# A two-block transformer on one core: modulation loads paced over four buffers, an earlier spread of inverse sums, squares added in two chains

## The chip, the core and the metric

One core of one Trainium2 chip runs the whole program. The metric is the device time of one execution in microseconds (us), taken as the median of several runs. TensorE (PE) multiplies, VectorE (DVE), ScalarE (ACT) and GpSimd (POOL) work elementwise, and DMA moves data. DMAs are issued from SyncE's queue (SP) or, here for some tensors, from POOL's. Each engine takes its instructions in order.

## What is computed

The input is 512 positions of width 1024, float32. The first model's two layers (A: attention over the 256 keys picked by an index score; B: attention with decay), each followed by an MLP, feed the second model's two layers (C: grouped attention; G: a gated MLP that mixes positions), again each with an MLP. Cut to what the change touches:

```python
def rms_norm(x, g):
    x32 = x.astype(jnp.float32)
    y = x32 * lax.rsqrt(jnp.mean(x32 * x32, axis=-1, keepdims=True) + EPS)
    return (y * g.astype(jnp.float32)).astype(x.dtype)
...
    cond = jax.nn.silu(c)                      # c: one vector of 1024
    for i in range(DEPTH):                     # two layers
        mod = cond @ ada_w[i] + ada_b[i]       # ada_w[i]: 1024 x 6144
        sh1, sc1, g1, sh2, sc2, g2 = jnp.split(mod, N_MOD, axis=-1)
...
        p = jax.nn.softmax(s, axis=-1).astype(v.dtype)
        return jnp.einsum('bkgqs,bskd->bqkgd', p, v)
```

`mod` depends on `c` alone, not on the positions, so the kernel computes it beside other work: layer 0's during the first model's first MLP, layer 1's during its second MLP.

## The kernel before, in words

**Layout.** The running state is eight tiles `h[0..7]`, 128 features by 512 positions each. Every product is done three times to keep float32 accuracy: each operand is split into a high part (ACT copies it to a rounded type) and a low part (DVE or POOL subtracts), and `mul3` (line 548) multiplies high by high, high by low and low by high. A weight tile (128x1024, 512 KB) is loaded by SP into `wr` (two buffers) and split into `wh` and `wl` (three buffers each).

**An MLP** (`mlp`, line 675) goes over four chunks of 1024 hidden features: eight "up" tiles, whose results pass through `t` (DVE), `a` (ACT), `ah` (ACT) and `al` (DVE), then eight "down" tiles, which read all eight `ah` and `al` and are added into `h` by DVE. A tile is 24 matmuls of 512 columns. In the first model's two MLPs, `step()` (line 681) advances a side task by one step after each tile but every eighth, 49 times in all; what is left of it is drained before the last eight down tiles.

**The side task** (`ada`, line 1236): for each of six column groups `q` and eight row blocks `k`, a 512 KB tile `adaw` of `ada_w` is loaded from POOL's queue, and DVE adds it, times one factor for each partition, into `ada` in two instructions of 512 columns. After the eighth, DVE transposes `ada` into another `adaw` buffer and reduces it into `red`. So one step is one load. At the end 16 small DMAs from POOL gather `red` into `part`, and DVE reduces that to `mod`. `adaw` has two buffers, the default of the MLP's pool.

**Attention heads** (`heads`, line 813) go two at a time. For each head, `softmax` (line 758) makes the logits in PSUM, DVE adds the mask and takes the extreme, and ACT takes the exponential and adds up the sums; `turned` (line 795) transposes on PE and splits; then matmuls with the values add up in the PSUM bank `po`. ACT and DVE bring `po` into `both`. In layers A and C (`late`) the division by the sums comes at the end: `inverses` (line 782) takes reciprocals on DVE, ACT spreads them over 64 columns each (into a tile of the tag `top`, one buffer), and PE transposes them into a `po` bank; then DVE multiplies `both`. The tag `po` has two banks. Layer A calls this 16 times (8 for the first 256 positions, with `narrow`, 8 for the others), layer C 8 times.

**Squares** (`squares`, line 583) serve `rms` (line 601) ahead of layer A, the first MLP, layer B and the second MLP: ACT squares the eight `h` tiles, and DVE adds seven of them one after the other into `acc`; four small matmuls with ones sum over the partitions.

**What sets the order.** The program is recorded, not emitted, by `Sched`. `order` (line 274) then plays a list schedule with its own costs (`cost`, line 243) and latencies: an instruction is placed when its inputs are there, its engine is free, its buffer is free (buffers of a tag are given out strictly in recorded order) and none of lower number is ready. The result is each engine's fixed order of instructions. On the chip the engines wait for one another by semaphores in that order, whatever the planner's clock said. `after` (line 194) adds one predecessor, the instruction recorded last, to all that is recorded within it; it is a predecessor in the planner alone, and the emitted program has no semaphore for it. All instructions are emitted at line 414, so the profile gives that one line and the rows are told apart by tile names.

```python
248:            return 1000 if o.eng == "gpsimd" else 60, 1550 + (x.box[1] - x.box[0]) * x.size * 4 / 360
262:            return (300 + 164 * n if n < 16 else 100 + 2.2 * n), 130
300:                if q["next"] != t.index or not room(t.pool, q):
685:                if side is not None and tiles % 8:
1245:                    w = self.t(pool, "adaw", [P, D])
1246:                    nc.gpsimd.dma_start(w, I["ada_w"][i, k, :, q * D : (q + 1) * D])
```

Line 248 books a load from POOL at 1000 ns of issue and 3006 ns to its landing for 512 KB.

Of the kernel before, what the change touches and what calls it, by code (L numbers as in the profile page):

```python
# [14 lines left out]
ALU = mybir.AluOpType  # L15
AX = mybir.AxisListType
PSUM = bass.MemoryType.PSUM

P = 128
S = 512  # L20
D = 1024
HALVES = slice(0, S // 2), slice(S // 2, S)
KD = D // P
# [15 lines left out]
V_BS = 208  # L39
V_QG, V_KG = 224, 226  # L40
NV = 228


class View:
# [110 lines left out]
class Sched:  # L155
# [37 lines left out]
    @contextmanager  # L193
    def after(self):

        self.gate = len(self.ops) - 1
        yield
        self.gate = None

# [42 lines left out]
    @staticmethod  # L242
    def cost(o, outs, ins):

        ps = any(x.tile.pool.space is not None for x in ins)
        if o.name == "dma_start":
            x = (outs + ins)[0]
            return 1000 if o.eng == "gpsimd" else 60, 1550 + (x.box[1] - x.box[0]) * x.size * 4 / 360
        n = max(x.size for x in outs + ins) if o.name in ("tensor_reduce", "bn_stats", "bn_aggr", "max") else outs[0].size
        if o.eng == "tensor":  # L250
            x = outs[0].size
            if o.name == "matmul" and ins[0].tile.dt == F32:
                return max(64, 4 * 0.42 * x), 200
            return max(107 if o.name == "transpose" else 54, 0.417 * x + 2.5), 200
        if o.eng == "scalar":
            aps = sum(isinstance(o.kw.get(k), View) for k in ("bias", "scale", "accum_out"))
            return (51 if ps else 93) + 0.834 * n + 93 * max(0, aps - 1) + (60 if aps == 1 else 0), 130
        if o.eng == "gpsimd":
            if o.name == "tensor_scalar":
                return 160 if n < 16 else 244 + 0.834 * n, 130  # L260
            if o.name == "memset":
                return 100, 130
            return (300 + 164 * n if n < 16 else 100 + 2.2 * n), 130
        c = 68 + 1.042 * n
        if o.name == "scalar_tensor_tensor" and isinstance(o.args[2], View):
            c += 61
        if o.name == "tensor_scalar" and not ps:
            c = 130 + 0.52 * n
        if o.name == "reciprocal":
            c = 70 + 6.3 * n  # L270
        return c, 130
# [219 lines left out]
class Net:  # L491
# [91 lines left out]
    def squares(self, col=None):  # L583

        nc = self.nc
        acc = self.t(self.np_, "acc", [P, S])
        for k in range(KD):
            kw = {} if col is None else {"scale": self.vec[:, col + k : col + k + 1]}
            sq = acc if k == 0 else self.t(self.np_, "sq", [P, S], bufs=1) if k % 2 else self.t(self.np_, "y", [P, S])
            nc.scalar.activation(sq, self.h[k], AF.Square, **kw)  # L590
            if k:
                nc.vector.tensor_tensor(acc, acc, sq, ALU.add)
        ps = self.po()
        for b in range(NB):
            nc.tensor.matmul(ps[:, 2 * b : 2 * b + 2], acc[:, b * P : (b + 1) * P], self.ones[:, 0:2], start=True, stop=True)
        return ps[:, 0 : 2 * NB : 2]
# [216 lines left out]
    def heads(self, pool, npr, nth, lhs, rhs, v, o, masks=None, causal=True, rows=(None, None), blocks=range(NB), narrow=False, late=False):  # L813


        nc = self.nc
        n = len(blocks) * P
        W = {i: (i + 1) * P if causal else S for i in blocks}
        keys = range(max(W.values()) // P)
        sums = self.t(pool, "sums", [P, 2 * len(blocks)])  # L820
        both = self.t(pool, "o", [P, n], bufs=1)
        for h in range(2):
            pr = self.softmax(pool, npr, lhs[h], rhs[h], W, masks, rows[h], sums, h, late)
            po = self.po()
            for b in keys:
                th, tl, c = self.turned(pool, nth, pr, W, b)
                if narrow:
                    for x, (part, y) in enumerate(((0, th), (0, tl), (64, th))):
                        nc.tensor.matmul(po[0:64, c], v[h][b][:, part : part + 64], y[:, c], start=b == 0 and x == 0, stop=b == keys[-1] and x == 2)
                else:  # L830
                    nc.tensor.matmul(po[:, c], v[h][b], th[:, c], start=b == 0, stop=False)
                    nc.tensor.matmul(po[:, c], v[h][b], tl[:, c], start=False, stop=b == keys[-1])
            r = slice(64 * h, 64 * h + 64)
            if narrow:
                nc.scalar.activation(both[r], po[0:64, :n], AF.Copy)
            else:
                top = self.t(pool, "top", [P, n], bufs=1)[0:64]
                nc.scalar.activation(top, po[0:64, :n], AF.Copy)
                nc.vector.tensor_tensor(both[r], po[64:128, :n], top, ALU.add)
        if late:  # L840
            nc.vector.tensor_tensor(both, self.inverses(pool, sums, len(blocks)), both, ALU.mult)
        self.split(o[0][:, :n], o[1][:, :n], both)

    def attn_out(self, o, w, gate=None, norm=None):
# [391 lines left out]
    def ada(self, i):  # L1236
        nc, I = self.nc, self.I

        def side(pool):
            m = self.mod[i]  # L1240
            red, part = (self.t(pool, x, [P, 4, 6 * KD], bufs=1) for x in ("red", "part"))
            for q in range(6):
                acc = self.t(pool, "ada", [P, D])
                for k in range(KD):
                    w = self.t(pool, "adaw", [P, D])
                    nc.gpsimd.dma_start(w, I["ada_w"][i, k, :, q * D : (q + 1) * D])
                    c = self.cs[:, k : k + 1]
                    for s in (0, 512):
                        a = acc[:, s : s + 512]
                        if k == 0:  # L1250
                            nc.vector.tensor_scalar(a, w[:, s : s + 512], c, 1.0, ALU.mult, ALU.mult)
                        else:
                            nc.vector.scalar_tensor_tensor(a, w[:, s : s + 512], c, a, ALU.mult, ALU.add)
                    if k < KD - 1:
                        yield

                tr = self.t(pool, "adaw", [P, D])
                nc.vector.transpose(tr, acc)
                nc.vector.tensor_reduce(red[:, :, q * KD : (q + 1) * KD], tr.rearrange("p (j a k) -> p a j k", a=4, k=32), AX.X, ALU.add)
                yield  # L1260
            for a in range(4):
                for g in range(4):
                    nc.gpsimd.dma_start(part[32 * a : 32 * a + 32, g, :], red[32 * g : 32 * g + 32, a, :])
                yield
            nc.vector.tensor_reduce(m, part.rearrange("p g k -> p k g"), AX.X, ALU.add)
            nc.vector.tensor_tensor(m, m, self.vec[:, V_ADAB[i] : V_ADAB[i] + 48], ALU.add)
            for col, g in ((8, V_N1[i]), (32, V_N2[i])):
                nc.vector.scalar_tensor_tensor(m[:, col : col + 8], m[:, col : col + 8], 1.0, self.vec[:, g : g + 8], ALU.add, ALU.mult)

        return side  # L1270
# [8 lines left out]
    def build(self):  # L1279
        nc, I = self.nc, self.I  # L1280
        self.vec = self.t(self.per, "vec", [P, NV])
        nc.sync.dma_start(self.vec, I["vec"])
# [87 lines left out]
def _layout(a):  # L1370
# [61 lines left out]
    r["vec"] = cat(cols, 1)  # L1432
    assert r["vec"].shape == (P, NV)
    r.update(_consts())
# [15 lines left out]
```

## Time and profile before

| | |
|---|---|
| median of 3 runs | 2618.81 us (2616.95 to 2618.96) |
| the profiled execution, its own time | 2615.0 us |
| its span, first to last instruction | 2613.2 us |
| mean granted TensorE clock | 0.992 |
| POOL busy, HBM read | 406.6 us (16%), 277.28 MB |
| chain that ended last, by engine | PE 77%, DVE 10%, DMA 7%, ACT 3%, issue 3% |

How to read it: the span is cut by the program into layer A (0 to about 261 us), the first MLP with the side task of layer 0 (to about 634), layer B (to about 880), the second MLP with the side task of layer 1 (to about 1240), layer C and its MLP (to about 1836), layer G and its MLP. PE is the engine to watch: wherever its share is full and its clock is at its full level, nothing else can shorten the run; where it falls short, something fed it late. A window of 50 us in which PE does nothing but 512-column matmuls back to back holds a fixed number of them, so a window's count shows what was lost there, both by idling and by a lower clock.

### The profile page before, as it was taken

The numbers are of one execution on the slowest core, as the hardware profiler recorded it, in microseconds if no ns is written. First come the engines' busy times: TensorE is split into PE (matmuls) and PEld (weight loads), VectorE is DVE, ScalarE is ACT, GpSimd is POOL, SyncE is SP. The second block draws the span as 40 slices with busy tenths as digits, with TensorE's granted clock in tenths as the row PEclk, the third lists the DMA queues.
The fourth block names the chain that finished last, engine by engine and source line by source line (L and its number), as shares of the span: only waits on it lengthen the run. The fifth ranks groups of instructions, "written<-read, shape, count | busy, mean of one in ns | idle before, by whom it ended". The sixth has DMA issues, their size and how long they took to land.

```text
span 2613.2 us, 33470 instructions
## 1 busy us (share of the span) xinstructions
PE 2544.9 (97%) x12614; PEld 2127.2 (81%) x12614; DVE 1582.8 (61%) x2629; ACT 1169.8 (45%) x2104; POOL 406.6 (16%) x453
## 2 busy tenths in 40 slices
PE   7999998999999998999999999999999999999999
PEld 6779786888888886888877888888888888888887
DVE  7998877445578778535698644435447654644433
ACT  5677322335488423324687523323425443523322
POOL 3741112000054111100541200001102110200000
PEclk9999998999999999999999999999999999999999
DMA  4222676333222577332310232222333322233232
GB/s 149 89 69 90 223 227 198 99 96 106 93 74 62 177 231 230 113 97 82 97 57 25 89 97 97 97 97 94 109 105 117 101 95 91 90 99 97 98 97 94
DMA packets 90419, 290.47 MB, mean 111 GB/s; under 512 B 12401, under 2 KB 15729, under 8 KB 90257
## 3 DMA queue, kind: packets, MB, share of 16 engines
q1 hardware_dynamic: 75408, 237.80, 28.3%
q0 software_dynamic: 14848, 50.54, 6.1%
q8 instruction: 99, 1.62, 0.2%
q14 instruction: 64, 0.52, 0.1%
HBM read 277.28 MB, written 2.10 MB: 107 GB/s over the span
## 4 chain that ended last, share of the span: by engine, by line
PE 77%; DVE 10%; DMA 7%; ACT 3%; issue 3%; POOL 0%; SPq 0%; DVEq 0%; ACTq 0%; POOLq 0%
PE mm L414 65%; DMA adaw<-in_ada_w 6%; PE lg L414 4%; PE tp L414 4%; PE po L414 3%; DVE ada L414 2%; DVE mask L414 1%; DVE wl L414 1%; DVE st L414 1%; DVE acc L414 1%; ACT wh L414 0%; DVE xl L414 0%; DVE y L414 0%; DVE o L414 0%; DVE pr L414 0%
## 5 line engine op out<-in xcount | busy, mean ns | idle before, releaser
L414 ACT ACTIVATE wh<-wr 128x1024 fp32r<-128x1024 f32 (+2 forms) x472 | 446.2, 951 | 1022.2 <-PE mm L414 847.3
L414 PE MATMUL mm<-xh,wh 128*128 128x512 f32 (+1 forms) x1640 | 625.7, 382 | 8.3 <-ACT wh L414 8.3
L414 DVE TENSOR_TENSOR wl<-wr,wh 128x1024 fp32r<-128x1024 f32 (+1 forms) x374 | 448.3, 1199 | 301.9 <-ACT wh L414 295.1
L414 PE MATMUL mm<-xh,wl 128*128 128x512 f32 (+1 forms) x1640 | 625.5, 382 | 5.4 <-DVE wl L414 4.8
L414 PE MATMUL mm<-xl,wh 128*128 128x512 f32 (+1 forms) x1640 | 625.0, 381 | 0.7 <-POOL xl L414 0.7
L414 PE MATMUL mm<-ah,wh 128*128 128x512 f32 (+1 forms) x1072 | 409.8, 382 | 13.7 <-ACT ah L414 13.7
L414 PE MATMUL mm<-al,wh 128*128 128x512 f32 (+1 forms) x1072 | 409.8, 382 | 3.6 <-DVE al L414 3.6
L414 PE MATMUL mm<-ah,wl 128*128 128x512 f32 (+1 forms) x1072 | 408.4, 381 | 0.6 <-DVE wl L414 0.6
L414 PEld LDWEIGHTS mm<-xh,wl 128*128 128x128 f32 x1640 | 311.3, 190 | 63.2 <-DVE wl L414 7.7
L414 PEld LDWEIGHTS mm<-xh,wh 128*128 128x128 f32 x1640 | 310.7, 190 | 62.4 <-ACT wh L414 8.7
L414 PEld LDWEIGHTS mm<-xl,wh 128*128 128x128 f32 x1640 | 311.4, 190 | 56.3 <-POOL xl L414 1.4
L414 PEld LDWEIGHTS mm<-ah,wh 128*128 128x128 f32 x1072 | 202.7, 189 | 54.2 <-ACT ah L414 15.8
L414 PEld LDWEIGHTS mm<-al,wh 128*128 128x128 f32 x1072 | 202.7, 189 | 44.5 <-DVE al L414 6.2
L414 DVE SCALAR_TENSOR_TENSOR h<-mm,mod,h 128x512 f32<-128x512 f32 (+1 forms) x113 | 79.9, 708 | 261.8 <-PE mm L414 261.6
L414 PEld LDWEIGHTS mm<-ah,wl 128*128 128x128 f32 x1072 | 202.8, 189 | 39.1 <-DVE wl L414 1.0
L414 POOL TENSOR_TENSOR wl<-wr,wh 128x512 fp32r<-128x512 f32 x98 | 132.5, 1362 | 220.6 <-ACT wh L414 215.8
L414 DVE SCALAR_TENSOR_TENSOR ada<-adaw,cs,ada 128x512 f32<-128x512 f32 x168 | 119.5, 748 | 72.5 <-DMA adaw<-in_ada_w 72.3
L414 ACT ACTIVATE pr<-pr,mn 128x128 f32<-128x128 f32 (+2 forms) x192 | 116.7, 610 | 21.0 <-DVE mn L414 20.2
L414 DVE TENSOR_TENSOR h<-mm,h 128x512 f32<-128x512 f32 (+1 forms) x91 | 56.3, 623 | 108.3 <-PE mm L414 108.2
L414 ACT ACTIVATE ah<-a 128x512 fp32r<-128x512 f32 x128 | 81.0, 632 | 83.8 <-DVE a L414 81.7
L414 DVE TENSOR_TENSOR al<-a,ah 128x512 fp32r<-128x512 f32 x128 | 88.2, 691 | 42.8 <-ACT ah L414 42.8
L414 PE MATMUL tp<-ident,pr 128*128 128x128 f32 x576 | 110.0, 277 | 1.9 <-ACT pr L414 1.0
(260 smaller groups left out, 3795.8 us busy)
## 6 DMA issues: line engine op xcount, KB each, us to landing
adaw<-in_ada_w POOLq DMA_DIRECT2D x96, 512.0 KB, 4.5
wr<-in_w_up SPq DMA_DIRECT2D x64, 512.0 KB
wr<-in_w_down SPq DMA_DIRECT2D x64, 512.0 KB
wr<-in_w_in SPq DMA_DIRECT2D x64, 512.0 KB
wr<-in_w_out SPq DMA_DIRECT2D x64, 512.0 KB
wr<-in_w_gu SPq DMA_DIRECT2D x24, 512.0 KB
wr<-in_w_gv SPq DMA_DIRECT2D x24, 512.0 KB
wr<-in_w_go SPq DMA_DIRECT2D x32, 384.0 KB
```

Source lines behind the costliest of these rows:

```text
L414: getattr(getattr(self.nc, o.eng), o.name)(*args, **kw)
```

## The change

Four edits go together. `ada`'s loads get four buffers in place of two, and the DVE instructions of a step get one more predecessor in the planner: the last instruction recorded before the step (the loads do not). The planner books loads from POOL at 600 ns of issue and 2000 ns more to their landing. In the late heads, `inverses` is recorded between the second head's softmax and its products, not after them; the multiplication stays where it was. `squares` keeps two sums: tiles 0, 2, 4, 6 and 7 on DVE, tiles 1, 3 and 5 on POOL, and one more DVE add joins them.

```diff
+AW = 4
...
     def after(self):
-        self.gate = len(self.ops) - 1
+        with self.paced(len(self.ops) - 1):
+            yield
+
+    @contextmanager
+    def paced(self, i):
+        self.gate = i
         yield
         self.gate = None
...
-            return 1000 if o.eng == "gpsimd" else 60, 1550 + (x.box[1] - x.box[0]) * x.size * 4 / 360
+            late = 1550 + (x.box[1] - x.box[0]) * x.size * 4 / 360
+            return (600, late + 2000) if o.eng == "gpsimd" else (60, late)
...
-        acc = self.t(self.np_, "acc", [P, S])
+        acc, acc2 = self.t(self.np_, "acc", [P, S]), self.t(self.np_, "acc", [P, S])
         for k in range(KD):
             kw = {} if col is None else {"scale": self.vec[:, col + k : col + k + 1]}
-            sq = acc if k == 0 else self.t(self.np_, "sq", [P, S], bufs=1) if k % 2 else self.t(self.np_, "y", [P, S])
+            a, eng, tag = (acc2, nc.gpsimd, "sq") if k in (1, 3, 5) else (acc, nc.vector, "y")
+            sq = a if k < 2 else self.t(self.np_, tag, [P, S], bufs=1 if tag == "sq" else None)
             nc.scalar.activation(sq, self.h[k], AF.Square, **kw)
-            if k:
-                nc.vector.tensor_tensor(acc, acc, sq, ALU.add)
+            if k > 1:
+                eng.tensor_tensor(a, a, sq, ALU.add)
+        nc.vector.tensor_tensor(acc, acc, acc2, ALU.add)
...
             pr = self.softmax(pool, npr, lhs[h], rhs[h], W, masks, rows[h], sums, h, late)
+            if late and h:
+                inv = self.inverses(pool, sums, len(blocks))
             po = self.po()
...
         if late:
-            nc.vector.tensor_tensor(both, self.inverses(pool, sums, len(blocks)), both, ALU.mult)
+            nc.vector.tensor_tensor(both, inv, both, ALU.mult)
...
                 for k in range(KD):
-                    w = self.t(pool, "adaw", [P, D])
+                    g = len(self.sched.ops) - 1
+                    w = self.t(pool, "adaw", [P, D], bufs=AW)
                     nc.gpsimd.dma_start(w, I["ada_w"][i, k, :, q * D : (q + 1) * D])
                     c = self.cs[:, k : k + 1]
-                    for s in (0, 512):
+                    with self.sched.paced(g):
+                        for s in (0, 512):
...
-                tr = self.t(pool, "adaw", [P, D])
-                nc.vector.transpose(tr, acc)
-                nc.vector.tensor_reduce(red[:, :, q * KD : (q + 1) * KD], tr.rearrange("p (j a k) -> p a j k", a=4, k=32), AX.X, ALU.add)
+                g = len(self.sched.ops) - 1
+                tr = self.t(pool, "adaw", [P, D], bufs=AW)
+                with self.sched.paced(g):
+                    nc.vector.transpose(tr, acc)
+                    nc.vector.tensor_reduce(red[:, :, q * KD : (q + 1) * KD], tr.rearrange("p (j a k) -> p a j k", a=4, k=32), AX.X, ALU.add)
```

## Rows read from the trace of the kernel before

**Rows 1.** The page: busy time of PE; DVE's busy tenths in 40 slices of 65 us.

```profile
PE 2544.9 (97%) x12614; PEld 2127.2 (81%) x12614; DVE 1582.8 (61%) x2629; ACT 1169.8 (45%) x2104; POOL 406.6 (16%) x453
...
DVE  7998877445578778535698644435447654644433
```

**Rows 2.** Windows: us, busy PE, PEld, DVE, ACT, POOL (x instructions), clock, DMA share, GB/s.

```profile
300.00:350.00 50.00, 46.73 (x199) 37.87 (x198) 37.40 (x50) 12.18 (x14) 7.39 (x14) 0.97 0.74 245
350.00:400.00 50.00, 46.24 (x202) 37.63 (x201) 37.22 (x50) 14.36 (x18) 6.87 (x13) 0.98 0.63 204
400.00:450.00 50.00, 44.41 (x176) 35.40 (x175) 38.68 (x51) 12.07 (x14) 8.37 (x17) 0.88 0.65 210
500.00:550.00 50.00, 50.00 (x222) 41.44 (x221) 17.91 (x19) 10.72 (x11) 0.00 (x0) 1.00 0.30 99
900.00:950.00 50.00, 48.51 (x213) 39.64 (x212) 41.57 (x55) 15.13 (x19) 7.38 (x14) 1.00 0.70 229
950.00:1000.00 50.00, 48.81 (x213) 39.50 (x213) 37.08 (x50) 13.22 (x16) 7.07 (x13) 1.00 0.68 223
1000.00:1050.00 50.00, 42.47 (x175) 33.42 (x174) 40.02 (x54) 13.20 (x17) 6.86 (x13) 0.93 0.71 230
```

**Rows 3.** The tile adaw: instructions (ns min/median/max), what ended its engine's idling, landing.

```profile
L414 DVE SCALAR_TENSOR_TENSOR ada<-adaw,cs,ada x168: 743/747/754, 266.3 to 1050.0; 128x512 f32<-128x512 f32 x168
...
L414 DVE STREAM_TRANSPOSE adaw<-ada x12: 1235/1245/1246, 294.3 to 1050.7; 128x1024 f32<-128x1024 f32 x12
L414 DVE TENSOR_REDUCE red<-adaw x12: 1199/1211/1220, 296.0 to 1052.0; 128x32 f32<-128x1024 f32 x12
...
  DMA adaw<-in_ada_w: 86.8, 66
...
DMA to landing us min/median/max: 3.9/4.5/8.2
```

**Rows 4.** Timeline of 312 to 316 us, first MLP: start, length, instruction [idle before <-releaser].

```profile
312.48 1.41 DVE L414 SCALAR_TENSOR_TENSOR ada<-adaw,cs,ada 128x512 f32<-128x512 f32 x2 [1.45 <-DMA adaw<-in_ada_w]
313.81 0.68 DVE L414 SCALAR_TENSOR_TENSOR t<-mm,y 128x512 f32<-128x512 f32 x1
...
315.19 0.63 ACT L414 ACTIVATE ah<-a 128x512 fp32r<-128x512 f32 x1
...
315.87 0.75 PE L414 MATMUL mm<-ah,wh 128*128 128x512 f32 x1 [3.27 <-ACT ah L414]
```

**Rows 5.** Timeline of 1437 to 1442 us, the last pair of heads of layer C.

```profile
1437.89 0.69 DVE L414 TENSOR_TENSOR o<-po,top 64x512 f32<-64x512 f32 x1 [1.38 <-ACT top L414]
1438.62 0.63 ACT L414 ACTIVATE top<-rs 128x512 f32<-128x512 f32 x1 [0.76 <-DVE o L414]
1439.30 0.66 PE L414 MATMUL po<-ident,top 128*128 128x128 f32 x4 [1.14 <-ACT top L414]
...
1441.40 0.97 PE L414 MATMUL mm<-st,wh 128*128 128x512 f32 x3 [1.45 <-ACT st L414]
```

**Rows 6.** Window behind that pair, columns as in rows 2.

```profile
1440.00:1450.00 10.00, 8.00 (x26) 5.97 (x27) 7.11 (x9) 4.31 (x6) 0.00 (x0) 0.83 0.21 61
```

**Rows 7.** Timeline of 1346 to 1350 us, a pair amid layer C: its first head's bank is emptied.

```profile
1347.44 0.58 ACT L414 ACTIVATE top<-po 64x512 f32<-64x512 f32 x1
...
1348.52 0.69 DVE L414 TENSOR_TENSOR o<-po,top 64x512 f32<-64x512 f32 x1
```

**Rows 8.** The tile acc: DVE's adds of squares from y (ns min/median/max).

```profile
L414 DVE TENSOR_TENSOR acc<-acc,y x12: 683/686/1666, 14.0 to 873.4; 128x512 f32<-128x512 f32 x12
```

**Rows 9.** The page's groups: POOL's instruction of the same form (busy us, mean ns).

```profile
L414 POOL TENSOR_TENSOR wl<-wr,wh 128x512 fp32r<-128x512 f32 x98 | 132.5, 1362 | 220.6 <-ACT wh L414 215.8
```

**Rows 10.** Timeline of 15 to 22 us, the squares ahead of layer A.

```profile
15.12 2.98 POOL L414 TENSOR_TENSOR wl<-wr,wh 128x512 fp32r<-128x512 f32 x2 [13.91 <-ACT wh L414]
...
16.99 1.67 DVE L414 TENSOR_TENSOR acc<-acc,y 128x512 f32<-128x512 f32 x1
...
21.03 1.05 PE L414 MATMUL po<-ones,acc 128*128 128x2 f32 x8 [1.10 <-DVE acc L414]
```

More of the change, by code (lines that the diff above doesn't have):

```diff
@@ L1244, in side @@
                 for k in range(KD):
-                    w = self.t(pool, "adaw", [P, D])
+                    g = len(self.sched.ops) - 1
+                    w = self.t(pool, "adaw", [P, D], bufs=AW)
                     nc.gpsimd.dma_start(w, I["ada_w"][i, k, :, q * D : (q + 1) * D])
                     c = self.cs[:, k : k + 1]
-                    for s in (0, 512):
[L1249 to L1253, printed above, removed]
+                    with self.sched.paced(g):
+                        for s in (0, 512):
+                            a = acc[:, s : s + 512]
+                            if k == 0:
+                                nc.vector.tensor_scalar(a, w[:, s : s + 512], c, 1.0, ALU.mult, ALU.mult)
+                            else:
+                                nc.vector.scalar_tensor_tensor(a, w[:, s : s + 512], c, a, ALU.mult, ALU.add)
                     if k < KD - 1:
                         yield
-                tr = self.t(pool, "adaw", [P, D])
-                nc.vector.transpose(tr, acc)
-                nc.vector.tensor_reduce(red[:, :, q * KD : (q + 1) * KD], tr.rearrange("p (j a k) -> p a j k", a=4, k=32), AX.X, ALU.add)
+                g = len(self.sched.ops) - 1
[3 more added lines that the diff above has]
+                    nc.vector.tensor_reduce(red[:, :, q * KD : (q + 1) * KD], tr.rearrange("p (j a k) -> p a j k", a=4, k=32), AX.X, ALU.add)
                 yield
```

## The prediction

> **What bounds the kernel now.** I read the page first. PE is busy for 97% of the span [rows 1], so only what PE loses can be won, and the question is where it loses. Next come the windows. In a stretch of an MLP without the side task (500 to 550 us), 50 us hold 222 matmuls of 512 columns at the full clock [rows 2], so one takes 50/222 = 0.225 us and a tile of 24 takes 5.4 us. In the first MLP the three windows that hold most of the side task are short of 222 by 23, 20 and 46, in the second MLP by 9, 9 and 47 [rows 2]. That is 154 matmuls, or 154 x 0.225 = **34.7 us**. It is made of idling (busy PE of 44.4 us, and 42.5 us in the worst window) and of the granted clock, which is 0.88 and 0.93 in the two worst windows: behind an idle stretch PE runs for some microseconds at 1.2 GHz, not 2.4. Both go if the idling goes.
>
> Why PE idles there is in the tile's view and the timeline. DVE sat idle 66 times, 86.8 us in all, until a load of adaw had landed [rows 3]. DVE takes its instructions in order, so what stands behind such a product waits too. At 312.48 DVE starts two products after 1.45 us of waiting; behind them stands t of the last up tile (313.81), behind that ACT's a and ah (315.19), and PE, which needs ah for the next down tile, starts at 315.87 after 3.27 us of idling [rows 4]. The planner did not see this coming: with 3006 ns to landing it put the product ahead of t, while the loads took 4.5 us in the median and up to 8.2 us [rows 3]. With two buffers the next load can't be sent before the last product but one is done, so each late load makes the next one late.
>
> **Part 1: pacing, and four buffers.** The products keep their number: 96 loads with two products each of at most 0.75 us, 12 transposes of 1.25 us and 12 reductions of 1.21 us [rows 3], 173 us in all, 86 us for one MLP. They now follow the step that they belong to, 49 steps over 56 tiles, that is 56 x 5.4 = 303 us in place of some 190 us. DVE was busy for 17.9 of 50 us without the side task [rows 2], 36%; with 86/303 = 28% more it comes to 64%, where the crowded windows had 74 to 83%. A tile leaves DVE 5.4 us, and t, which follows, is due only when the next tile ends. Behind a paced product stand t, wl and al of the next tile, and the reader after them is PE; a product that starts right behind al of its own tile is over 1.5 us later, long before the next t. The tile that ends an up chunk has no step behind it, and the longest steps, with transpose and reduction, fall on tiles 9, 18, 27, 36, 45 and 54, none of them the last of an up chunk.
>
> Are the loads early enough? A load may go when its buffer is free, three to four tiles (16 to 22 us) ahead of its use, against 8.2 us for the slowest landing [rows 3]. The transposed copy takes one of the four buffers, so at a change of column group the planner gives the next load out only one tile ahead; there it now books 0.6 + 5.0 = 5.6 us and puts the products behind that, while POOL really sends earlier. The predecessor itself makes no wait on the chip; it only sets places in the order. POOL has nothing behind a load that waits: the adds of squares, which now pass through its queue, are recorded ahead of the MLP, and the fifth load follows the first tile's products. SP's queue of weights is not passed by anything. The 16 small DMAs of the end move from near 450 us to the end of the fourth up chunk, with eight down tiles (43 us) over them. I take **-33 us**: 34.7 less 1.7 for small waits that remain at the MLP's start, where up to four loads come at once. Bounds: -35, and -17 if half of the waits stay.
>
> Here a rule speaks against the edit. In the crowded windows the 16 DMA engines were busy for up to 0.74 and moved up to 245 GB/s [rows 2]. The Trainium skill, DMA: Bandwidth & Descriptors, "Issuing engines are not separate DMA queues", says that transfers issued from different engines run on the same 16 engines and interleave. By that rule four buffers bring no bandwidth, and if the transfers were the bound the waits would only move; it stands below as the first rival. By the rows they are not: 48 loads of 0.52 MB in 303 us are 83 GB/s, which with the 99 GB/s of the weights [rows 2] make 182, under the 204 to 245 already reached.
>
> **Part 2: the spread ahead of the second head's products.** At the end of layer C nothing hides the chain: DVE's add ends at 1437.89 + 0.69 = 1438.58, then come ACT's spread (0.63) and four transposes until 1439.96, and only then the multiplication; PE idles 1.14 and 1.45 us [rows 5], and in the window behind it the clock is 0.83 [rows 6]. With the transposes done before, the multiplication starts 1.38 us earlier. Bounds: nothing (the spread now stands in front of th on ACT and may delay the products by its 0.63 us), and 2.6 us of idling plus 0.17 x 10 = 1.7 us of clock, 4.3 us. I take **-2 us**. In the other 23 pairs the same shorter chain could give up to 1.38 us each, but the spread now holds one of the two po banks while the second head's products run. These must wait until the first head's bank is empty, 1347.44 to 1348.52 + 0.69 = 1349.21, or 1.77 us in a busy stretch [rows 7]. Before, that wait came once in a pair (the next pair's first head, behind the spread); now it comes twice, each time shorter. DVE is busy for 8 to 9 tenths in these layers [rows 1] and gets neither more nor less work, and PE has projections and output products to fill in. Over layers A and C I take **0**, between -5 and +18.
>
> **Part 3: squares in two chains.** DVE has five adds of 0.69 us [rows 8] in place of seven, POOL two of 1.36 us [rows 9]. In three of the four places PE is full, with three PSUM tiles to fill before the result is needed. Ahead of layer A, PE waited 1.10 us for acc [rows 10]; two adds less on DVE's chain are worth about that, so **-1 us**, with the bounds -2 and +3. Against it: an add on DVE took 1.67 us beside a POOL subtraction, where the median is 0.69 [rows 8, 10], so POOL's two adds can each hold DVE up by about 1 us.
>
> The Trainium skill, SBUF — State Buffer, "Who interferes with whom", states it as a rule: a DVE instruction with two SBUF inputs and a GpSimd instruction that reads SBUF exclude each other, and the later one waits for the whole of the other. The row of 1.67 us agrees. By the rule alone, with eight POOL adds all in DVE's way, part 3 would be +8 us and the sum 2591.
>
> **Sum.** -33 - 2 - 1 = -36 us against the profiled execution's own 2615.0 us: 2579. That execution lies 3.8 us below the median of the runs shown and 2.0 below the lowest; I carry 3 of it, which gives **2582 us**.
>
> **The rivals.** *Loads remain late (12%).* If the transfers or their start, not the order, were the bound, half of the waits would stay: 2582 + 17 = 2599. For it: DMA shares of 0.63 to 0.74 [rows 2]. Against it: the 245 GB/s reached. *The bank costs something (10%).* If 0.75 us of the second bank wait is exposed in each of 24 pairs, that is +18: 2600. *Slower (5%).* The same mechanism in full: 24 x 1.77 = 42 us on top, 2624. It decides from 36/24 = 1.5 us exposed per pair. For it: PE and DVE are both nearly full in layer C, so an empty slot is lost to both. Against it: the wait before was just as long and PE had work. *Attention gains too (8%).* The end of layer C gives its whole 4.3 us and the other pairs 0.4 us each: 2570. *The edit does nothing (3%).* The gate exists in the planner alone; if buffers and lower numbers already set the same order, the time is 2618.
>
> **How the numbers follow.** The forecast, 2574 to 2591, has 62%. The first two rivals and part of the fourth lie within 2568 to 2604; what is left out is the slower case, the edit without effect and the edges of the others, some 17%. This kernel's measurement tells 0.2%, about 5 us, from no change. Faster by more: 62 + 12 + 10 + 8 = 92%; within it 3%; slower 5%.
>
> **What would show it.** Step 1 is right if the windows from 300 to 450 and 880 to 1050 hold 220 matmuls or more at a clock of 1.00, the side task's products reach to about 560 us, and DVE's idling until adaw falls from 86.8 us to under 15. Step 2 shows as multiplication right behind the add at layer C's end, and as layers A and C being as long as before within 5 us. Step 3 shows as PE's wait for acc near 20 us under 0.5 us. I am wrong if these windows stay short of 222, or if po products in layer C wait for DVE's o and the layer grows.

## The result, and the profile after

The changed kernel takes **2597.2 us** in the median (2595.03 to 2599.67) beside 2617.88 us of the kernel before on the same chip: a ratio of 0.9922 (95% interval 0.9904 to 0.9939), 20.7 us less. The forecast was 2582 us, 36 less. The direction held; the size did not, by 15 us: 2597.2 lies outside the forecast's own 2574 to 2591, and inside 2568 to 2604 only because that takes in the first two rivals.

The page first, with the lines that answer to [rows 1]: PE has 98% of a span of 2593.5 us (2613.2 before).

```profile
PE 2540.0 (98%) x12614; PEld 2131.7 (82%) x12614; DVE 1589.1 (61%) x2621; ACT 1168.3 (45%) x2104; POOL 416.4 (16%) x461
...
DVE  7998766665478666666698534445447554634433
```

DVE's line is flat in the two MLPs where it had peaks. The windows show what that did, with the columns of [rows 2]:

```profile
300.00:350.00 50.00, 50.00 (x222) 41.39 (x222) 31.97 (x41) 14.53 (x18) 4.61 (x9) 1.00 0.57 183
350.00:400.00 50.00, 50.00 (x222) 41.39 (x221) 34.16 (x44) 17.54 (x23) 4.23 (x8) 1.00 0.56 182
400.00:450.00 50.00, 50.00 (x222) 41.42 (x221) 31.30 (x39) 11.55 (x13) 4.23 (x8) 1.00 0.57 187
...
900.00:950.00 50.00, 50.00 (x222) 41.41 (x221) 32.23 (x41) 13.08 (x16) 4.22 (x8) 1.00 0.55 179
950.00:1000.00 50.00, 50.00 (x222) 41.41 (x221) 34.78 (x44) 18.80 (x25) 4.22 (x8) 1.00 0.55 179
1000.00:1050.00 50.00, 50.00 (x223) 41.38 (x222) 29.53 (x37) 10.72 (x11) 4.22 (x8) 1.00 0.56 183
```

Each holds the full 222 matmuls at a clock of 1.00, also those that held 176 and 175. The loss of the MLPs is gone as a whole. The tile adaw says why; beside [rows 3], look for the line of the DMA among what ended DVE's idling:

```profile
L423 DVE SCALAR_TENSOR_TENSOR ada<-adaw,cs,ada x168: 741/744/747, 289.4 to 1163.7; 128x512 f32<-128x512 f32 x168
...
  DVE ada L423: 465.9, 78
  DVE red L423: 28.7, 10
  PE mm L423: 0.9, 1
...
DMA to landing us min/median/max: 3.9/4.4/9.1
```

There is none: 86.8 us of idling until a load had landed have become 0. (The 465.9 us are POOL's: its loads wait for a buffer.) The loads land no sooner, 4.4 us in the median, 9.1 at most; they are sent earlier.

So, by the count of matmuls, some 35 us were won in the MLPs, and some 14 lost elsewhere: in the traces layer A ends at 270.2 us in place of 261.6, and layer C takes 236.7 us in place of 232.3. The timeline of layer C's last pair of heads, beside [rows 5]:

```profile
1418.40 0.69 DVE L423 TENSOR_TENSOR o<-po,top 64x512 f32<-64x512 f32 x1 [1.42 <-ACT top L423]
1419.13 0.69 DVE L423 TENSOR_TENSOR o<-po,o 128x512 f32<-128x512 f32 x1
1419.86 0.63 ACT L423 ACTIVATE st<-o 128x512 fp32r<-128x512 f32 x1 [1.49 <-DVE o L423]
...
1420.54 1.23 PE L423 MATMUL mm<-st,wh 128*128 128x512 f32 x3 [2.33 <-ACT st L423]
```

The multiplication stands right behind the add, as forecast. From the add's start to PE's next output product it is 2.14 us (1418.40 to 1420.54) against 3.51 us. But PE's idling only shrank from 1.14 + 1.45 to 2.33 us, and the window behind has the clock of before, 0.83 (columns of [rows 6]):

```profile
1420.00:1430.00 10.00, 9.46 (x33) 7.17 (x34) 7.59 (x9) 5.22 (x7) 0.00 (x0) 0.83 0.33 106
```

Amid layer C there is a wait that the trace of before does not have. The timeline of one pair, where the first head's bank is emptied:

```profile
1327.51 0.61 ACT L423 ACTIVATE top<-po 64x512 f32<-64x512 f32 x1
...
1328.56 0.69 DVE L423 TENSOR_TENSOR o<-po,top 64x512 f32<-64x512 f32 x1
...
1329.49 0.60 ACT L423 ACTIVATE q<-mm 128x512 f32<-128x512 f32 x1
1330.12 0.63 ACT L423 ACTIVATE top<-rs 128x512 f32<-128x512 f32 x1
...
1330.80 0.66 PE L423 MATMUL po<-ident,top 128*128 128x128 f32 x4 [1.56 <-ACT top L423]
...
1331.75 0.48 PE L423 MATMUL po<-th,v 128*128 128x512 f32 x1
```

DVE empties the first head's bank until 1329.25. The spread (top<-rs) writes the tile top, which that add has just read, and follows on ACT behind q<-mm; PE idles 1.56 us for it, and the second head's first product stands behind the four transposes in PE's order. Last, the squares ahead of layer A, beside [rows 10]:

```profile
13.91 1.29 POOL L423 TENSOR_TENSOR acc<-acc,sq 128x512 f32<-128x512 f32 x1 [12.70 <-DMA wr<-in_w_qi]
...
14.38 4.76 DVE L423 TENSOR_TENSOR acc<-acc,y 128x512 f32<-128x512 f32 x3 [0.35 <-ACT y L423]
...
15.47 1.42 POOL L423 TENSOR_TENSOR wl<-wr,wh 128x512 fp32r<-128x512 f32 x1 [0.27 <-ACT wh L423]
...
16.84 1.75 POOL L423 TENSOR_TENSOR acc<-acc,sq 128x512 f32<-128x512 f32 x1
...
18.74 3.21 POOL L423 TENSOR_TENSOR wl<-wr,wh 128x512 fp32r<-128x512 f32 x2
...
19.25 1.58 DVE L423 TENSOR_TENSOR acc<-acc,acc 128x512 f32<-128x512 f32 x1
...
20.88 1.05 PE L423 MATMUL po<-ones,acc 128*128 128x2 f32 x8 [1.37 <-DVE acc L423]
```

DVE has fewer adds, but three in a row take 4.76 us, 1.59 each, and the last 1.58, where one alone takes 0.69 [rows 8]. All of them lie beside POOL's five instructions. PE's wait for acc rose from 1.10 to 1.37 us; the forecast was under 0.5.

### The profile page after: what moved, and what is told of

It reads as the page before. It is cut to its first block, busy times and chain, and to the rows that moved or that the text cites. A ratio compares the mean times of both kernels' runs of the same rounds, so it can differ in the third digit from the quotient of the medians.

```text
span 2593.5 us, 33435 instructions
## 1 busy us (share of the span) xinstructions
PE 2540.0 (98%) x12614; PEld 2131.7 (82%) x12614; DVE 1589.1 (61%) x2621; ACT 1168.3 (45%) x2104; POOL 416.4 (16%) x461
## 5 line engine op out<-in xcount | busy, mean ns | idle before, releaser
L423 POOL DMA_DIRECT2D adaw<-in_ada_w x96 | 51.1, 533 | 495.6 <-DVE ada L423 465.9
```

The costliest lines, as they stand in the source:

```text
L423: getattr(getattr(self.nc, o.eng), o.name)(*args, **kw)
```

## The experiments

The theory after the result: pacing is worth all that was forecast; the early spread costs, since it holds a po bank; and the adds on POOL cost, by their work and not by the second chain. The rival: each part does what was forecast, and pacing gave less.

### Each part alone

e1 takes the modulation's edits only, e2 the early spread only, e3 the squares only, each on the kernel before. e4 is e3 with both chains on DVE:

```diff
-            a, eng, tag = (acc2, nc.gpsimd, "sq") if k in (1, 3, 5) else (acc, nc.vector, "y")
+            a, eng, tag = (acc2, nc.vector, "sq") if k in (1, 3, 5) else (acc, nc.vector, "y")
```

> The kernel before with the pacing, the four buffers and the planner's new cost of POOL's loads alone. Theory (the three parts add up; pacing gives all it was forecast to give, the other two parts give some back): layers A and C as long as before (261.6 and 232.3 us), the two MLPs with the side task some 20 and 15 us shorter, the whole 34 us under the kernel before, ratio 0.987. Rival (the parts hang together, and layers A and C lengthen because the planner's order of the whole program moved): layer A near 270 us here too and a ratio near 0.992.

> The kernel before with the spread of the inverse sums ahead of the second head's products alone. Theory (the po bank that the spread holds makes heads wait): layer A longer by 4 to 7 us and layer C by 3 to 5 us, nothing else moved, the whole slower by 7 to 12 us. Rival (the squares on POOL are what layer A lost): layer A within 1 us of 261.6, layer C longer by 4 us, the whole slower by 4.

> The kernel before with the squares in two chains, one of them on POOL, alone. Theory: layer A longer by 2 to 4 us (the acc is no earlier, since POOL's adds and splits and DVE's adds exclude each other, and the weight splits on POOL are later), all other stages within 1 us, the whole slower by 2 to 4 us. Rival (squares are what layer A lost): layer A longer by 8 us and the whole slower by 8.

> The kernel before with the squares in two chains, but both on DVE, so that POOL has none of the adds. If what squares cost in layer A comes from POOL's adds (DVE and POOL in each other's way, weight splits on POOL later), layer A is within 1 us of 261.6 here. If it comes from the shape of two chains and the reordering that it brings, layer A is longer by 2 to 4 us here too.

Against 2617.34 us before:

| run | median us | ratio (95%) | difference us |
|---|---|---|---|
| e1 | 2583.66 | 0.9867 (0.9851 to 0.9884) | -33.7 |
| e2 | 2627.59 | 1.0039 (1.0024 to 1.0054) | +10.2 |
| e3 | 2623.85 | 1.0023 (1.0013 to 1.0033) | +6.5 |
| e4 | 2614.89 | 0.9995 (0.9985 to 1.0005) | -2.5 |

Pacing gave its 33 us; the rival is out. Both other parts slow the kernel down. Two chains on DVE cost nothing that these runs can tell; having POOL add to one does cost. The parts add up to -17.0, the whole change measured -20.7; the 3.7 us between them are within the measurement.

### The early spread: is it the bank?

e5 has pacing, the early spread in all pairs, and a third po bank; e6 pacing and the third bank; e11 pacing and the early spread with the two banks of the change. e7 has pacing and the early spread in layer C's last pair alone. All four have the squares of before.

```diff
-        return self.t(self.pp, tag, [P, S], F32, {"mm": 3, "lg": 3, "tp": 3, "po": 2}[tag])
+        return self.t(self.pp, tag, [P, S], F32, {"mm": 3, "lg": 3, "tp": 3, "po": 3}[tag])
```

```diff
-            if late and h:
+            if early and h:
                 inv = self.inverses(pool, sums, len(blocks))
...
-                self.heads(pool, 3, 2, [(q, q) for q in st], [kd[n]] * 2, [[x[:, n, :] for x in v]] * 2, o[j], [zero] * NB, causal=False, late=True,
+                self.heads(pool, 3, 2, [(q, q) for q in st], [kd[n]] * 2, [[x[:, n, :] for x in v]] * 2, o[j], [zero] * NB, causal=False, late=True, early=j == KD - 1,
```

> Pacing and the earlier spread (squares as before), with three po banks in place of two. Bank theory (the spread holds a bank, so the second head's products wait until the first head's bank is empty): with a third bank nothing waits, layers A and C are within 2 us of pacing alone (263.6 and 233.7 us) and the whole is 2580 to 2585. Rival (PE, which takes its work in order, now stands at the transposes until reciprocals and spread are done, and the planner's order around them is worse): the third bank changes nothing, layer A stays 5 us and layer C 4 us longer, the whole 2590 to 2595.

> Pacing alone with three po banks in place of two: the control for the run with the earlier spread. Bank theory: the spread is late here and holds a bank only shortly, so layers A and C move by less than 2 us against pacing alone (263.6 and 233.7). If layer A or C gets shorter or longer by more, the third bank has an effect of its own and the run with the spread is to be read against this one.

> Pacing, and the earlier spread in the last pair of layer C alone. Both theories: the end of layer C keeps its one idle stretch of some 2.3 us in place of 1.1 and 1.4, the multiplication follows the add directly; with no pair behind it, no bank and no position in PE's order is lost. Layer C is 231 to 233 us against 233.7 with pacing alone, the whole 2581 to 2584, which is within what three rounds tell of pacing alone.

> The control for e5 on its own ground: paced modulation and the early spread in all pairs, with the two po banks of the change. If the second bank held by the spread is what costs, 8 to 12 us above pacing alone (2592 to 2596 us). If the early spread costs nothing beside pacing and the third bank brought nothing in e5, 2584 to 2587 us.

| run | median us | before us | ratio (95%) | difference us |
|---|---|---|---|---|
| e5, spread early, three banks | 2585.27 | 2616.68 | 0.9877 (0.9855 to 0.9898) | -31.4 |
| e6, three banks | 2583.76 | 2616.68 | 0.9870 (0.9849 to 0.9892) | -32.9 |
| e7, last pair only | 2582.09 | 2616.68 | 0.9865 (0.9843 to 0.9887) | -34.6 |
| e11, spread early, two banks | 2594.03 | 2617.96 | 0.9903 (0.9890 to 0.9917) | -23.9 |

With two banks the early spread takes back 9.8 us of pacing's 33.7; with three, 1.5 of 32.9, which can't be told from nothing. The third bank alone gives nothing. The intervals of e5 and e11 overlap at their ends, but all four runs of e5 (up to 2586.84 us) lie below all four of e11 (from 2589.23). So the cost goes with a third bank, though the spread's place on ACT, the transposes and `top`, the spread's other tile with its one buffer, stay as they are. (The planner writes another order when it has one bank more; that is a part of what the bank does.)

Where is it lost? Layer C, from PE's last product of the second MLP to its last output product, takes 231.4 to 234.6 us in the ten traces where the spread is late (e7's, with its one early pair, among them); 236.7, 237.9 and 239.6 in the changed kernel, e2 and e11; and 229.5 in e5. The third sixth of layer C, in windows with the columns of [rows 2]: e1, with the late spread,

```profile
1287.20:1326.20 39.00, 38.71 (x216) 30.80 (x215) 36.64 (x78) 35.36 (x81) 13.97 (x10) 1.00 0.15 46
```

e11, with the early spread and two banks,

```profile
1293.60:1333.50 39.90, 35.93 (x184) 28.26 (x182) 34.73 (x66) 30.66 (x67) 11.21 (x8) 0.91 0.14 40
```

and e5, with three:

```profile
1289.80:1328.10 38.30, 37.28 (x206) 29.17 (x206) 37.38 (x77) 31.97 (x73) 13.90 (x10) 1.00 0.15 45
```

In e11 PE idles 4.0 of 39.9 us, and the clock is 0.91; in the other two it is 1.00. Of the 4.0 us, 1.6 are for a spread, at 1330.01, as in the changed kernel above. The others, 0.9 for mn, 1.1 for sqh and 0.3 for msh, lie between 1295 and 1301 us, where the second head's products of the first pair are missing. The timeline of e11,

```profile
1238.04 0.27 PE L423 MATMUL po<-ident,rf 128*128 128x128 f32 x1
...
1282.75 0.60 PE L423 MATMUL po<-ident,top 128*128 128x128 f32 x4
...
1294.78 0.49 PE L423 MATMUL po<-ident,rf 128*128 128x128 f32 x3
...
1298.95 0.59 ACT L423 ACTIVATE y<-po 128x512 f32<-128x512 f32 x1
...
1301.37 0.63 PE L423 MATMUL po<-th,v 128*128 128x512 f32 x1
```

and of e5:

```profile
1280.88 0.60 PE L423 MATMUL po<-ident,top 128*128 128x128 f32 x4
1281.24 0.48 PE L423 MATMUL po<-th,v 128*128 128x512 f32 x1
```

rf holds the scales of a norm, which the kernel spreads over a po bank of its own, at low priority. PE writes the first block of it at 1238.04 and the last three at 1294.78, and ACT has read it at 1298.95 + 0.59 = 1299.54. Until then the heads have one of the two banks. The early spread takes that one at 1282.75, so the second head's products start only at 1301.37, 18 us behind the transposes. With three banks they stand right behind them. In e1, where the spread comes after both heads, one bank is enough: the second head's products start at 1277.24, 0.9 us after the first head's bank is empty.

So in layer C the loss is not spread over the pairs. It is a few idle stretches in the early pairs and the slow clock behind them; between 1334 and 1420 us e11 shows one wait of PE, of 0.4 us. Between e1 and e11 layer C accounts for some 6 of the 9.8 us. Where the others go is not shown. Layer A ends at 269.6, 267.1 and 267.1 us in e2, e5 and e11, and at 261.4 to 263.6 in the kernel before, e1, e7 and e12, which would be a loss that the third bank leaves; but it ends at 267.3 in e8 too, where the spread is late. Single traces don't tell: the last MAX8 of layer A's top-k, up to which all engines have one and the same order of work in these kernels, starts at 171.6 us before, at 172.4 in e1, 170.6 in e7 and 175.7 in e8.

e7, which keeps the early spread only where nothing follows it, is 0.9 us below e1, in the direction of the forecast 2 us but within the measurement.

### The squares: POOL's work, or another order?

e8 has pacing and the changed squares everywhere but ahead of layer A, where the one chain of before stands.

```diff
-        r, rb = self.rms()
+        r, rb = self.rms(two=False)
```

e9 and e10 separate the engine from the order. The planner orders the program with the adds on one engine, and they are emitted on the other, at the same places. e9 is e3, planned for POOL and run on DVE; e10 is e4, planned for DVE and run on POOL. The edit of e9 (e10's puts the two adds on "gpsimd"):

```diff
                 eng.tensor_tensor(a, a, sq, ALU.add)
+                if k in (3, 5):
+                    self.sched.put[len(self.sched.ops) - 1] = "vector"
...
-                getattr(getattr(self.nc, o.eng), o.name)(*args, **kw)
+                getattr(getattr(self.nc, self.put.get(o.i, o.eng)), o.name)(*args, **kw)
```

> Pacing, and the squares in two chains, one on POOL, everywhere but ahead of layer A. If the squares cost what they cost in layer A, where POOL splits the weights: all stages within 2 us of pacing alone, the whole 2581 to 2586. If they cost at each of the four places (DVE and POOL in each other's way): each MLP or layer behind them longer by 1 to 2 us, the whole 2586 to 2590.

> The kernel before with the squares in two chains, ordered as if POOL did the adds of tiles 3 and 5 (every engine's order as in e3), but the two adds are emitted on DVE. If it is POOL's work itself that costs (its place between the halves of the weight split, or POOL and DVE shutting each other out of SBUF), the 6.5 us of e3 go and the time is that of before, within 3 us, with layer A near 262 us. If it is the other order that the planner then writes for all of layer A, the cost stays: 6 to 9 us slower than before, layer A near 270 us.

> The reverse: ordered as in e4, where DVE does all adds and nothing was lost, but the adds of tiles 3 and 5 are emitted on POOL at the same places of the order. If POOL's work itself costs, 5 to 9 us slower than before; if the order costs, the time of e4, within 3 us of before.

e8: 2583.45 us beside 2616.68, ratio 0.9864 (0.9837 to 0.9891), -33.2, as pacing alone, but the interval leaves some 7 us to either side. The traces are closer: from the last MAX8 of layer A to PE's last product of the second MLP, a stretch that holds the other three places, e8 takes 1037.7 us, e1 1036.9 and e7 1037.0. So the squares cost ahead of layer A; in the other three places they cost under 1 us. e9 and e10 beside 2617.96 us before:

| adds planned on, run on | median us | ratio (95%) |
|---|---|---|
| DVE, DVE (e4) | 2614.89 | 0.9995 (0.9985 to 1.0005) |
| POOL, DVE (e9) | 2621.13 | 1.0007 (0.9998 to 1.0015) |
| DVE, POOL (e10) | 2622.62 | 1.0018 (1.0009 to 1.0027) |
| POOL, POOL (e3) | 2623.85 | 1.0023 (1.0013 to 1.0033) |

Running them on POOL costs in either order: 0.0023 of the time (6 us) from e4 to e10, where the intervals are apart, and 0.0016 (4 us) from e9 to e3, where they touch. The other order may cost 0.0005 to 0.0012 (1 to 3 us), which these runs can't tell from nothing. The traces don't exclude it: the last MAX8 of layer A starts at 181.4 us in e3, 178.2 in e10 and 176.0 in e4, but at 179.9 in e9 too, where POOL has none of the adds, against the 170.6 to 175.7 of one chain. What POOL's adds do shows where the order is the same. The window of 16 to 32 us and PE's row for acc in e4,

```profile
16.00:32.00 16.00, 15.25 (x73) 11.96 (x73) 10.40 (x16) 7.69 (x14) 11.11 (x9) 1.00 0.40 117
...
19.12 1.05 PE L414 MATMUL po<-ones,acc 128*128 128x2 f32 x8
```

and in e10, with DVE's adds:

```profile
16.00:32.00 16.00, 12.60 (x53) 9.39 (x52) 9.34 (x14) 7.20 (x14) 9.29 (x8) 0.89 0.26 82
...
15.70 4.76 DVE L415 TENSOR_TENSOR acc<-acc,y 128x512 f32<-128x512 f32 x3 [0.35 <-ACT y L415]
...
20.56 1.57 DVE L415 TENSOR_TENSOR acc<-acc,acc 128x512 f32<-128x512 f32 x1
...
22.18 1.24 PE L415 MATMUL po<-ones,acc 128*128 128x2 f32 x8 [2.04 <-DVE acc L415]
```

With all adds on DVE, PE does not wait for acc at all. With two on POOL, DVE's own four take 6.33 us (4.76 + 1.57) where four of 0.69 would take 2.76; PE waits 2.04 us and does 15.25 - 12.60 = 2.7 us less work in the window, at a clock of 0.89. The clock can't be put down to the adds: the same window of the kernel before has 0.89 as well, and that of e3, the slowest of the four runs, has 1.00, in this order:

```profile
16.00:32.00 16.00, 14.07 (x62) 11.16 (x62) 9.39 (x15) 6.81 (x13) 8.14 (x7) 0.89 0.38 101
16.00:32.00 16.00, 14.11 (x69) 11.00 (x68) 10.58 (x13) 5.74 (x11) 10.87 (x8) 1.00 0.38 108
...
20.76 1.05 PE L414 MATMUL po<-ones,acc 128*128 128x2 f32 x8 [1.37 <-DVE acc L414]
```

In e3 PE waits 1.37 us for acc and does 1.1 us less work than in e4. So it is shown that POOL's adds lengthen DVE's chain and that PE waits for it, 1.4 to 2.0 us; where the rest of the some 6 us goes is not.

### What of the modulation's edits does it?

e12 has the four buffers and nothing else: no added predecessor, the planner's old price of a load.

```diff
-                    w = self.t(pool, "adaw", [P, D])
+                    w = self.t(pool, "adaw", [P, D], bufs=4)
...
-                tr = self.t(pool, "adaw", [P, D])
+                tr = self.t(pool, "adaw", [P, D], bufs=4)
```

> The kernel before with four buffers for adaw and nothing else: no added predecessor, the old cost of a load. If the order is what matters (the planner puts a product as early as it believes the load to have landed, 3.0 us after its issue, where it takes 4.5), DVE still idles until adaw for more than 40 us and the time stays within 15 us of before, 2600 to 2618 us. If the buffers alone set the loads early enough, most of the 33.7 us of pacing come: 2584 to 2592 us, and DVE's idling until adaw is under 20 us.

2579.73 us beside 2615.98, ratio 0.9858 (0.9833 to 0.9884), -36.3 us: the buffers alone give all of it. The windows of the first MLP,

```profile
300.00:350.00 50.00, 50.00 (x223) 41.40 (x222) 47.88 (x66) 12.52 (x14) 9.71 (x19) 1.00 0.87 294
350.00:400.00 50.00, 50.00 (x222) 41.44 (x221) 48.65 (x66) 19.59 (x25) 7.78 (x15) 1.00 0.78 265
```

and the tile adaw (what ended its engines' idling, and the landing):

```profile
  DMA adaw<-in_ada_w: 10.0, 9
...
DMA to landing us min/median/max: 3.9/5.1/7.7
```

The side task is as crowded as before, and more: DVE is busy for 48.65 of 50 us. PE still loses nothing, because DVE no longer stands still in front of t: 10.0 us of idling are left of 86.8. e12 and e7 (2582.09) are both faster than the changed kernel, and e12 is the lowest of all, though e1, e7 and e12 can't be told apart by their intervals. The simplest of the best versions is thus the four buffers alone, the only part of the change that was needed.

## Why the prediction was right and wrong

**Part 1, -33 us: right, and for a part of its reason.** e1 gave -33.7. The windows from 300 to 450 and 880 to 1050 hold 222 matmuls, DVE's idling until adaw is 0, and the products of the first MLP run to 570.8 us, where the section on what would show it asked for about 560. The count of missing matmuls (154 x 0.225 us) was the right measure. But I put the gain on the new order, 303 us of pacing in place of 190, and worked out DVE's share to see that it fits. e12 shows that the paced order is not needed: four buffers let POOL send loads ahead, and DVE may be full. The sentence of the prediction that carried it was the other one, that with two buffers each late load makes the next one late.

**The first rival** (transfers are the bound) is out twice: by e1, and by e12, where the DMAs move 294 GB/s with PE full. The Trainium skill, DMA: Bandwidth & Descriptors, "Issuing engines are not separate DMA queues", says that queues of different engines share the same 16 DMA engines; the trace agrees in so far as their share rises to 0.87, but that was not yet the limit. That the 2597.2 us measured lie 2 us from this rival's 2599 is chance: its condition did not come about.

**Part 2, -2 us: wrong; this is the step that failed first.** With pacing it measured +9.8 (e11 against e1), alone +10.2. At layer C's end the chain became 1.37 us shorter, close to the 1.38 forecast; what that brings, 0.9 us by e7, can't be told from nothing. The failed step is "over layers A and C I take 0" for the other 23 pairs: they measured some +10. Some 6 us of it are seen in layer C. The second wait for a bank stood there, and as a rival at 10%, "the bank costs something"; in size that rival is what came about, with +10 in place of +18, but not in its form, 0.75 us in each pair. The prediction gave the heads both banks and let the second head wait 1.77 us for the first one's. In the first pair of layer C the scales rf hold one bank, and the second head's products come 18 us late. I dismissed the wait with "PE has projections and output products to fill in". They filled most of those 18 us; 2.3 us of idling remained there and 1.6 in a later pair, at a clock of 0.91 in e11's window. A price for each pair times 24 was the wrong form of the sum: in layer C a few pairs pay, the others next to nothing. For layer A it is open.

**Part 3, -1 us: wrong sign.** Alone it measured +6.5, on top of the others +3.2 (e11's -23.9 against -20.7, which is within the measurement). Two adds less on DVE's chain were to shorten it by what PE waits, 1.10 us. I had the counterweight in the text, DVE's adds beside POOL take 1.67 us, and counted it as about 1 us for each POOL add, then set it aside for the sum. In fact all four DVE adds behind the first ran beside POOL, at 1.58 to 1.59 us each. The Trainium skill, SBUF — State Buffer, "Who interferes with whom", says that a DVE instruction with two SBUF inputs and a GpSimd instruction that reads SBUF shut each other out; the rows of 4.76 us for three adds agree. By that rule alone the prediction gave +8, near to the +6.5 of the part alone. The nearness is luck: the +8 counted eight POOL adds over four places, and the cost lies at one place with two of them. But the row I had, 1.67 us, had the sign right, and the sum should have gone by it. The failed step is "two adds less on DVE's chain are worth about that": PE's wait for acc became 1.37 us in place of 1.10.

**The sum.** -33.7 + 9.8 + 3.2 = -20.7. Forecast -33 - 2 - 1 = -36. Of the 15 us, 12 are part 2, 4 part 3, and pacing gave back 1. Two of the three parts had the wrong sign; the direction held because the first is so much larger.

## What to carry to other kernels

When a side task makes a full engine wait, try more buffers for its loads before any new order: here depth alone gave the whole gain, and the paced order nothing more. Before a result is computed earlier, ask what it holds meanwhile, a bank above all, who else holds one of the same tag, and look at the first repetitions of the loop too, not only at one in the middle. Moving work to an idle engine is no gain where that engine's instructions stop the one they were meant to relieve; and a change of several parts that is faster as a whole can hold parts that are slower, which only a run of each part shows.

## What the runs showed of the hardware that I had not expected

DVE adds of two SBUF tiles beside busy POOL: some 1.6 us each (1.57 to 1.59 in the rows above), 2.3 times the 0.69 of one alone, for as long as POOL had such work. DMAs: 294 GB/s over 50 us at a share of 0.87, above the 245 GB/s seen before, with loads still landing in 5.1 us in the median. Up to the end of layer A's top-k, executions with the same order of work on every engine were up to 5.1 us apart (170.6 to 175.7), so a few us in one trace of that layer prove nothing.
